# Both mixers of a two-layer encoder, ordered by the scheduler's other machine model

## The chip, the cores and the metric

The kernel runs on one core of one Trainium2 chip. The metric is the device time of one execution in microseconds. The core has five instruction streams that run side by side and meet at semaphores: TensorE (PE in the profile; PEld is its weight load), VectorE (DVE), ScalarE (ACT), GpSimd (POOL), and SyncE (SP), which issues all the DMAs here. Each of them takes its instructions in the order in which the compiled program lists them.

## The reference

The model is an encoder trunk with two layers on one sequence of 1024 tokens, each of 1024 float32 numbers. Each layer is a mixer and a SwiGLU, both with an RMSNorm ahead of them and a residual sum behind them.

```python
h = x
for layer in range(2):
    u = rms_norm(h, g_mix[layer])
    h = h + (mla_stick_breaking_mixer if layer == 0 else chunk_band_mixer)(u, ...)
    u = rms_norm(h, g_ffn[layer])
    h = h + (silu(u @ w_gate) * (u @ w_up)) @ w_down
return rms_norm(h, g_final)
```

The first mixer has two groups of eight heads. One group is latent attention (MLA): queries and keys come out of low-rank products with their own norms, and a rotary part is added; the softmax sees whole chunks of 64 tokens up to its own. The other is stick-breaking attention, strictly causal, without a softmax:

```python
log_keep = where(before, log_sigmoid(-z), 0)
log_between = cumsum(log_keep, reverse=True) - log_keep
w = where(before, exp(log_sigmoid(z) + log_between), 0)
```

The second mixer is attention with sixteen heads in which each chunk of 64 tokens sees itself and the eight chunks before it, with a learned bias per head and distance.

## The kernel before, in words

Everything is kept transposed, model dimension on the 128 partitions, tokens along the free dimension, in two halves of 512 tokens. A matrix product in nearly float32 precision is made of three products of rounded parts: `mm3` (L277 to L282) multiplies high by high, high by low and low by high, each a TensorE instruction of up to 512 columns. The parts come from `split` (L250): the high part is a rounding copy (`round_to`, L243, ScalarE or VectorE), the low part a subtraction (`rest`, L248, on VectorE or GpSimd as the caller says). `weight` (L267) loads a tile of weights from DRAM (L264) and splits it; `dense` (L284) is a row of `mm3` into one PSUM bank.

The program has four stages.

*The first mixer* (`mixer0`) starts with `start` (L351): for each of the 16 tiles of x a load, the scaled high part and low part (`feed`, L327 and L328), the value products of all heads, and the query and key products of the first two heads. Then come four rounds of stick-breaking attention, two heads each (`sb_step`): scores (L894, L895), a chain over VectorE, ScalarE and GpSimd (L897 to L904, with `rest` for the low part), the running sums as products with a triangle of ones (L916 to L921), the weights (L927, L928) and the products with the values (`weighted`, L831). Beside the rounds run the projections for later heads. Beside the fourth round runs `prepare`: the latent projections, their two norms (`feed`, `square_sum` L299 to L303, `rstd` L313 to L320, `columns` L343), the rotary part (L988 to L990), the first heads' keys (L1002, L1005) and the maximum of the first heads' scores (L1049, L1051; L1030, L1033, L1035). Then come four rounds of MLA attention (`mla_attend`, scores L1120 to L1122, exponentials L1123, sums L1072, denominators L1088) with the next heads' projections beside them, and the output projection (`out_half`) of the first half of the tokens beside the last round.

*The SwiGLU stages* (`ffn`) compute the hidden layer and the way down by a seven-product scheme (`Seven`). The second half of the mixer's output projection runs at their head. Their instructions are written out by hand as a list of steps.

*The second mixer* (`mixer1`) has eight rounds of two heads (`band_project`, `band_max` with L1175 and L1178, `band_attend` with L1201 to L1204), with the projections of later heads beside them.

**What sets the order.** Two things. In the code, `weave` (L785) draws from two generators, attention steps and dense products, by costs that are written by hand, and `step` (L764) puts a step's later parts behind the first parts of later steps: this gives the order in which the program is traced. Then, when the `TileContext` closes, the framework's scheduler plays the traced program on a model of the machine. For each engine it takes, among the instructions whose inputs are done and whose buffer is free at that moment of the model, the one that was traced first. So an instruction that the model sees as late is passed by others of its engine. The order that comes out for each engine is the program; buffers of a pool are handed out on the way. Costs of instructions enter through the model alone.

The body of each SwiGLU stage is exempt: inside `with self.pinned()` (L231) every instruction of TensorE, VectorE, ScalarE and GpSimd gets an edge to the one traced before it on its engine, so these keep the traced order:

```python
class PinnedCore:
    def __init__(self, tc):
        nc = tc.nc
        self.sync = nc.sync
        self.tensor, self.vector, self.scalar, self.gpsimd = (
            Pinned(tc, e) for e in (nc.tensor, nc.vector, nc.scalar, nc.gpsimd))
```

SyncE's DMAs are not wrapped, so their order is the scheduler's in all four stages. Behind the pinned body, each SwiGLU stage ends with the products of its last group (`add`, L706), which is scheduled freely, together with the head of what follows.

The function that the change touches is `kernel`, the last of the file:

## Time and profile before

| | us |
|---|---|
| three timed runs | 2590.89, 2594.2, 2595.98 |
| their median | 2594.2 |
| the profiled execution | 2591.68 |
| its span, first to last instruction | 2589.5 |

The profile is of one execution. "Busy" is the union of the records of an engine's instructions; records of TensorE overlap, since a product's record opens before the one ahead of it has closed. A line of groups gives the source line, the engine, what is written and read by the names in the code, shapes and count, then busy us and mean ns, then the idle time of the engine just before these instructions and what ended it. A line L243, L248 or L280 is that of a helper; L74 is the helper through which every pinned instruction is traced. The granted clock is TensorE's, as a share of full speed.

The stages lie at 0 to about 645 us (first mixer), to about 1340 us (first SwiGLU), to about 1880 us (second mixer), and to the end (second SwiGLU and the final norm).

### The profile page before, as it was taken

How to read it: one execution, taken by the hardware profiler on the slowest of the kernel's cores; microseconds unless marked ns; L12 is line 12 of the kernel's file. 1: busy time of each engine (PE TensorE's matmuls, PEld its weight loads, DVE VectorE, ACT ScalarE, POOL GpSimd, SP SyncE). 2: the span in 40 equal slices, each digit the busy share in tenths (PEclk: the TensorE clock that was granted, in tenths of full speed). 3: DMA queues.
4: the chain of work that ended last, by engine and by line, in shares of the span. 5: the costliest groups of instructions: out<-in, count | busy, mean ns of one | idle time of the engine just before them, and what ended most of it. 6: DMA issues, size and time to landing. Idle time of an engine off the chain costs nothing.

```text
span 2589.5 us, 33647 instructions
## 1 busy us (share of the span) xinstructions
PE 2513.1 (97%) x11758; PEld 1938.4 (75%) x11758; DVE 1890.9 (73%) x3072; ACT 1168.4 (45%) x2028; POOL 517.0 (20%) x489
## 2 busy tenths in 40 slices
PE   7999989999999999999999999999999999999997
PEld 6766766557778888888877777776777888888886
DVE  6888887665787666677765777777688766667776
ACT  4777676444454334433252433334444443444324
POOL 3333324653000000000031333335300000000004
PEclk9999999999999999999999999999999999999999
DMA  4221100124434344476652222223553434447661
GB/s 143 61 60 54 54 17 29 35 74 153 162 100 160 109 143 143 139 260 209 227 168 68 74 74 86 74 70 91 178 167 99 165 105 140 145 137 262 210 226 69
DMA packets 179432, 319.70 MB, mean 123 GB/s; under 512 B 20544, under 2 KB 36800, under 8 KB 179264
## 3 DMA queue, kind: packets, MB, share of 16 engines
q1 hardware_dynamic: 179264, 317.56, 37.2%
q8 instruction: 93, 1.52, 0.2%
q14 instruction: 75, 0.61, 0.1%
HBM read 222.58 MB, written 84.41 MB: 119 GB/s over the span
## 4 chain that ended last, share of the span: by engine, by line
PE 73%; DVE 8%; DMA 2%; ACT 1%; issue 1%; POOL 0%; DVEq 0%; SPq 0%; POOLq 0%; ACTq 0%
PE z L74 24%; PE mm L74 12%; PE o L74 6%; PE mm L280 6%; PE mm L281 6%; PE mm L282 6%; PE o L831 4%; DVE u L74 2%; PE z L1201 2%; PE z L1175 1%; PE z L1202 1%; PE z L1120 1%; DVE u L303 1%; PE z L1088 1%; PE z L1121 1%
## 5 line engine op out<-in xcount | busy, mean ns | idle before, releaser
L74 PE MATMUL z<-u,vh 128*128 128x512 f32 x976 | 304.0, 393 | 4.6 <-DVE u L74 4.6
L74 PE MATMUL z<-u,wh 128*128 128x512 f32 x976 | 302.2, 390 | 6.4 <-DVE u L74 6.4
L280 PE MATMUL mm<-u,wh 128*128 128x512 f32 x720 | 291.7, 405 | 2.9 <-DVE c L989 1.8
L281 PE MATMUL mm<-u,wh 128*128 128x512 f32 x720 | 284.1, 395 | 0.9 <-DVE u L248 0.9
L248 POOL TENSOR_TENSOR wl<-wr,wh 128x512 fp32r<-128x512 f32 (+2 forms) x95 | 122.0, 1289 | 809.2 <-ACT wh L243 739.0
L282 PE MATMUL mm<-u,wl 128*128 128x512 f32 x720 | 282.9, 393 | 0.0
L74 PE MATMUL mm<-u,wh 128*128 128x512 f32 x720 | 223.4, 392 | 4.5 <-ACT wh L74 4.5
L74 PEld LDWEIGHTS z<-u,wh 128*128 128x128 f32 x976 | 183.2, 188 | 47.3 <-DVE u L74 9.5
L74 PEld LDWEIGHTS z<-u,vh 128*128 128x128 f32 x976 | 184.4, 189 | 45.4 <-ACT u L74 6.2
L74 PE MATMUL z<-u,vl 128*128 128x512 f32 x488 | 191.1, 392 | 0.0
L74 PE MATMUL z<-u,wl 128*128 128x512 f32 x488 | 189.9, 389 | 0.0
L280 PEld LDWEIGHTS mm<-u,wh 128*128 128x128 f32 x720 | 135.5, 188 | 64.8 <-issue 40.3
L831 PE MATMUL o<-a,u 128*64 128x512 f32 (+3 forms) x768 | 171.8, 483 | 0.2 <-ACT a L1204 0.2
L74 PEld LDWEIGHTS mm<-u,wh 128*128 128x128 f32 x720 | 134.7, 188 | 35.7 <-ACT wh L74 6.9
L281 PEld LDWEIGHTS mm<-u,wh 128*128 128x128 f32 x720 | 135.8, 189 | 31.0 <-issue 6.8
L282 PEld LDWEIGHTS mm<-u,wl 128*128 128x128 f32 x720 | 135.6, 188 | 29.2 <-issue 2.1
L74 PE MATMUL mm<-u,vh 128*128 128x512 f32 x496 | 152.7, 389 | 0.0
L248 POOL TENSOR_TENSOR u<-wr,u 128x512 fp32r<-128x512 f32 x8 | 10.9, 1374 | 668.6 <-ACT u L243 668.6
L74 PE MATMUL mm<-u,wl 128*128 128x512 f32 x360 | 140.8, 391 | 0.8 <-DVE wl L74 0.5
L1204 ACT ACTIVATE a<-a 128x1024 f32<-128x1024 f32 (+3 forms) x96 | 70.6, 738 | 144.6 <-DVE a L1203 144.4
L74 ACT CAST vh<-vr 128x512 fp32r<-128x512 f32 (+1 forms) x166 | 95.9, 577 | 80.2 <-DVE vr L74 31.2
L1203 DVE TENSOR_TENSOR a<-z,bias 128x1024 f32<-128x1024 f32 (+3 forms) x96 | 78.8, 823 | 70.1 <-PE z L1202 54.7
(248 smaller groups left out, 5968.5 us busy)
## 6 DMA issues: line engine op xcount, KB each, us to landing
u<-f_t SPq DMA_DIRECT2D x144, 256.0 KB, 5.2
vr<-in_w_up SPq DMA_DIRECT2D x88, 256.0 KB, 4.2
wr<-in_w_gate SPq DMA_DIRECT2D x88, 256.0 KB, 3.6
f_t<-x SPq DMA_DIRECT2D x72, 256.0 KB, 2.0
wr<-in_w_out SPq DMA_DIRECT2D x64, 256.0 KB, 3.0
f_t<-e SPq DMA_DIRECT2D x54, 256.0 KB, 3.5
ld<-f SPq DMA_DIRECT2D x54, 256.0 KB, 5.2
h<-u SPq DMA_DIRECT2D x48, 256.0 KB, 2.4
```

Of the source, the lines that this page charges most:

```text
L74: return lambda *a, **k: self.tc.keep_in_program_order(f(*a, **k))
L248: self.eng(eng).tensor_tensor(lo, src, hi.bitcast(F32), ALU.subtract)
L280: mm(out, wh, xh, start=first, stop=False, skip_group_check=onto)
L281: mm(out, wh, xl, start=False, stop=False, skip_group_check=onto)
L282: mm(out, wl, xh, start=False, stop=last, skip_group_check=onto)
L303: self.eng(eng).tensor_tensor(acc, acc, sq, ALU.add)
L831: self.nc.tensor.matmul(o[rh, cs], vt[j // 4][:, j % 4, rh], w[:, e, cs], start=first, stop=last)
L1088: nc.tensor.matmul(den[64 * e:64 * e + 64, :], self.ones[:, 0:64], esum[:, e, :], start=True, stop=True)
L1120: mm(z[:, e, cs], kth[0:kr, bs], qh[0:kr, cs], start=True, stop=False)
L1201: mm(z[:, e, cs], ks[e][kh][0][:, bs], qs[e][hf][0][:, cs], start=True, stop=False)
L1203: nc.vector.tensor_tensor(ex[:, :, cs], z[:, :, cs], tk[:, :, xs], ALU.add)
L1204: nc.scalar.activation(ex[:, :, cs], ex[:, :, cs], AF.Exp)
```

## The change

The scheduler can play the program on either of two models of the machine. The default is used before; the other, a simulator of the engines' timelines, is chosen by one argument. It models with its own costs what an instruction takes, when its result can be used, how many instructions wait ahead of an engine, when a DMA lands, what a GpSimd operation takes, and TensorE's clock. The traced program is the same; the order of each engine's list and the handing out of buffers are the scheduler's under that model, wherever the code does not pin them.

```diff
-    with tile.TileContext(nc) as tc:
+    with tile.TileContext(nc, schedule_with_timeline_sim=True) as tc:
         tile_trunk(tc, args)
```

## The prediction

> **What bounds the kernel now.** I read the page first, then the busy time of each engine by stage, then what TensorE waited for, then ten-microsecond windows where its idle time is bunched. From the page, the span, the busy times and the engine shares of the chain of waits:
>
> ```profile
> span 2589.5 us, 33647 instructions
> ...
> PE 2513.1 (97%) x11758; PEld 1938.4 (75%) x11758; DVE 1890.9 (73%) x3072; ACT 1168.4 (45%) x2028; POOL 517.0 (20%) x489
> ...
> PE 73%; DVE 8%; DMA 2%; ACT 1%; issue 1%; POOL 0%; DVEq 0%; SPq 0%; POOLq 0%; ACTq 0%
> ```
>
> TensorE (PE) is busy 2513.1 of 2589.5 us, so all its idle time is 76.4 us, and VectorE (DVE) is the only other engine with a real share of the chain. An order of instructions adds and removes no work; what it can move is those 76.4 us, and how much new idle time it makes. Where they lie, by stage (start:end, length, then busy us and instructions of PE, PEld, DVE, ACT, POOL, granted TensorE clock, DMA share, GB/s):
>
> ```profile
> core 0: us, PE busy (x) PEld busy (x) DVE busy (x) ACT busy (x) POOL busy (x), PEclk, DMA share, GB/s
> 0.00:60.00 60.00, 45.65 (x264) 39.40 (x265) 41.46 (x50) 27.02 (x49) 24.98 (x25) 1.00 0.48 145
> 60.00:340.00 280.00, 273.30 (x1338) 199.29 (x1336) 240.62 (x306) 192.56 (x284) 98.95 (x127) 1.00 0.20 58
> 340.00:440.00 100.00, 89.12 (x349) 59.51 (x348) 85.79 (x106) 68.62 (x121) 37.40 (x31) 0.91 0.07 20
> 440.00:645.00 205.00, 199.30 (x878) 125.31 (x878) 130.65 (x167) 94.04 (x148) 109.59 (x76) 1.00 0.26 81
> 645.00:750.00 105.00, 98.16 (x416) 75.93 (x413) 89.06 (x141) 50.31 (x87) 0.00 (x0) 0.98 0.36 118
> 750.00:1160.00 410.00, 410.00 (x1810) 339.50 (x1809) 279.98 (x454) 168.82 (x310) 0.00 (x0) 1.00 0.47 162
> 1160.00:1260.00 100.00, 97.39 (x428) 80.01 (x428) 77.94 (x141) 32.67 (x66) 0.00 (x0) 1.00 0.66 227
> 1260.00:1340.00 80.00, 77.27 (x340) 62.66 (x339) 55.24 (x84) 33.80 (x58) 24.08 (x23) 1.00 0.55 178
> 1340.00:1880.00 540.00, 537.50 (x2871) 391.44 (x2870) 382.92 (x795) 212.05 (x375) 190.93 (x181) 1.00 0.30 91
> 1880.00:1980.00 100.00, 93.23 (x390) 73.01 (x389) 86.83 (x138) 48.42 (x84) 0.00 (x0) 0.98 0.35 118
> 2400.00:2500.00 100.00, 98.02 (x432) 80.54 (x431) 75.50 (x138) 30.38 (x61) 0.00 (x0) 1.00 0.62 214
> 2500.00:2590.00 90.00, 74.12 (x411) 64.00 (x409) 56.17 (x92) 36.17 (x71) 31.05 (x27) 0.95 0.33 111
> ```
>
> The first mixer (0 to 645 us) holds 14.4 + 6.7 + 10.9 + 5.7 = 37.6 us of the idle time, the second (1340 to 1880 us) only 2.5. The SwiGLU stages have no idle time in their long middle (750 to 1160 us) and 6.8 us at each start (645 to 750 and 1880 to 1980), the same twice, in instructions that are held in program order. What TensorE waited for, in total us, times and longest:
>
> ```profile
> PE z L282 <- DVE u L328: 7.3, 6, 1.7
> PE z L280 <- ACT wh L243: 5.8, 1, 5.8
> PE mm L280 <- DVE f L989: 3.5, 1, 3.5
> PE z L921 <- POOL c L248: 2.9, 4, 1.1
> PE z L1088 <- DVE b L1072: 2.9, 2, 1.5
> PE z L1033 <- DVE m L1030: 2.6, 1, 2.6
> ```
>
> These are small waits of one to three microseconds at the head of an in-order list: an instruction stands ahead of others although its operand is late. That is what another order can change. The 5.8 is the first load of the kernel, and stays.
>
> **The change part by part.** It removes and adds no instruction and no byte. It replaces the order of TensorE, VectorE, ScalarE and GpSimd in both mixers, in the last products of each SwiGLU stage (outside the pinned part), and of the DMA issues of SP everywhere, since those are pinned nowhere; buffers are handed out in the new order too. I price it stage by stage by the idle time, with both ends: all of a stage's idle time goes, or as much is added as a row of this trace shows for a stage of its kind.
>
> *Start, 0 to 60 us: idle 14.4 us, taken as -1.* Half of it is the first load and the ramp, 7.3 us are the six waits of the value products for the low part `u` of L328. Each low part hangs on a load, a cast and a subtraction that no order shortens; only another product can be put in front. Ends: -7 and +4 (half of it again).
>
> *Stick-breaking, 60 to 340 us: idle 6.7 us, taken as -3.* The waits for `c` of L248 and its like are about one microsecond each and have dense products as neighbours that could go first, so a model that knows the low part later puts them first. Ends: -6.7 and +6.7.
>
> *The latent projections, 340 to 440 us, taken as -4.* Here is the largest single piece:
>
> ```profile
> 300.00:310.00 10.00, 10.00 (x50) 8.11 (x49) 5.81 (x7) 5.21 (x7) 2.15 (x4) 1.00 0.17 53
> 310.00:320.00 10.00, 10.00 (x53) 7.93 (x50) 5.88 (x9) 5.24 (x9) 3.87 (x6) 1.00 0.12 38
> 320.00:330.00 10.00, 10.00 (x48) 7.37 (x48) 6.68 (x11) 5.70 (x10) 2.59 (x5) 1.00 0.08 27
> ...
> 360.00:370.00 10.00, 9.87 (x39) 6.50 (x38) 9.91 (x14) 6.80 (x10) 2.48 (x2) 1.00 0.00 0
> 370.00:380.00 10.00, 9.65 (x37) 5.31 (x36) 9.78 (x13) 7.70 (x12) 2.57 (x2) 1.00 0.01 2
> 380.00:390.00 10.00, 3.79 (x13) 2.21 (x12) 9.42 (x14) 6.36 (x10) 4.17 (x4) 0.60 0.00 0
> 390.00:400.00 10.00, 9.93 (x41) 7.51 (x41) 7.59 (x10) 8.55 (x22) 2.33 (x2) 0.88 0.23 72
> ...
> 420.00:430.00 10.00, 7.19 (x21) 5.58 (x22) 8.54 (x13) 5.12 (x9) 4.72 (x5) 0.66 0.07 20
> ```
>
> From 360 to 390 us VectorE is busy 29.1 of 30 us and TensorE loses 0.1 + 0.4 + 6.2 = 6.7 us behind it; from 300 to 330 us VectorE was busy only 18.4 of 30 us with TensorE full. So it is a bunching of VectorE work, not a lack of VectorE time. The idle time costs a second time: the granted clock falls to 0.60, 0.88 and 0.66, and the busy time in these three windows is worth 3.79 x 0.40 + 9.93 x 0.12 + 7.19 x 0.34 = 5.1 us less than at full clock. The stage is thus worth 10.9 + 5.1 = 16 us. An order can spread the bunch (-16) or make another like that of 360 to 400 us (6.7 + 1.5 + 1.2, about +9). A greedy order does not look ahead to the bunch, so I take a quarter of the gain.
>
> [...]
>
> *MLA attention, 440 to 645 us: idle 5.7 us, taken as -2*, by the argument of the stage before last. Ends: -5.7 and +5.7.
>
> *Second mixer, 1340 to 1880 us: idle 2.5 us, taken as +2.* There is next to nothing to win here. The cover is TensorE's own queue of ready dense products; if the new order has the share of idle time that 60 to 340 us has (2.4%), it is 12.9 us, +10.4 against now. Ends: -2.5 and +10.4; I take the low side because VectorE is busy only 382.9 of 540 us there.
>
> *The issues of SP, taken as 0.* Their waits, in total us, times and longest:
>
> ```profile
> SPq L264 <- POOL wl L248: 346.6, 88, 20.0
> SPq L264 <- DVE wl L248: 239.5, 66, 42.0
> ```
>
> The weight loads wait for their buffers, so a changed issue order mostly changes where SP waits. Behind a waiting load stand the moves of queries and keys and the loads of attention outputs. In the SwiGLU stages only 1160 to 1260 and 2400 to 2500 us have idle time in reach of a late load: 2.6 + 2.0, ends -4.6 and +4.6. The starts of those stages and the kernel's end I leave as they are: pinned, or a last chain that no order shortens.
>
> The sum is -1 - 3 - 4 - 2 + 2 + 0 = -8 us. The profiled execution took 2591.68 us (span 2589.5 and 2.2 around it), so it would take 2583.7; the median of the three timed runs is 2594.2, 2.5 us above the profiled one, so I predict 2586 for the median.
>
> **The rivals.** *The waits only move (2594).* As many waits arise as go, or the order hardly differs, since most of each engine's sequence is set by data and buffers and the SwiGLU stages are pinned; this is also the case in which the change does not do what it says. For it: every stage's gain above is a few microseconds, and the second mixer's +10.4 would by itself cancel the sum. Against it: the waits of the first mixer have ready neighbours.
>
> *Slower: VectorE bunches more (2613).* The mechanism is that of 360 to 400 us: VectorE serves attention steps, splits and the norm and rope chain from one in-order list, and an order that puts the chain's instructions where attention needs VectorE most makes TensorE wait and its clock fall. A piece costs about 9.4 us; two more pieces and none of the gains make 2594 + 19 = 2613. For it: VectorE is busy 240.6 of 280 and 85.8 of 100 us from 60 to 440 us, so it has 54 us to spare beside 18 of TensorE's. Against it: the spare time just before the bunch. It decides as soon as one piece comes without the sum's gain.
>
> A row that speaks to VectorE's length in any order, two groups of one operation and shape, from 60 to 645 us:
>
> ```profile
> L248 DVE TENSOR_TENSOR c<-b,c 128x512 fp32r<-128x512 f32 x24 | 24.3, 1014 | 2.4 <-ACT c L904 2.3
> L248 DVE TENSOR_TENSOR wl<-wr,wh 128x512 fp32r<-128x512 f32 x35 | 23.9, 691 | 3.7 <-ACT wh L243 3.5
> ```
>
> The `c` subtraction runs while GpSimd does the other half of the same pair, and takes 1014 ns for 691. An order that sets 24 such pairs apart in time saves VectorE 24 x 0.32 = 8 us, one that brings as many other subtractions beside GpSimd costs it as much; either is inside the ends of the stages. [...]
>
> *Larger gain (2566).* The bunch spreads wholly (-16) and the waits of 60 to 340 and 440 to 645 us go (-6.7 - 5.7): 2594 - 28 = 2566. For it: the spare VectorE time. Against it: that everything would have to go right at once.
>
> *Slower by TensorE's own order (about 2610).* From the page:
>
> ```profile
> L831 PE MATMUL o<-a,u 128*64 128x512 f32 (+3 forms) x768 | 171.8, 483 | 0.2 <-ACT a L1204 0.2
> ```
>
> The half-array products of L831 now overlap in twos: 768 records of 483 ns are 371 us, in 171.8 us of time. If one in ten of these 384 twos lost its overlap, that would be 38 x 0.4 = 15 us more. Nothing in the data forces the two apart, and they are neighbours in the code, so this is the least likely.
>
> **How the numbers follow.** Chances: the forecast 0.32, the larger gain 0.12, moved waits 0.21, VectorE's bunches 0.25, TensorE's order and others on that side 0.10. A measurement of this kernel can tell about 0.2%, 5.2 us, from no change: faster 0.44, the same 0.21, slower 0.35. The likeliest case alone runs from 2575 to 2589. The ends of all stages together are about -42 and +40 us; since they will not all fall to one side, and no more than 2 in 10 is to be left out, the range is 2564 (the larger gain) to 2622 (three bunches and no gain).
>
> **What would show it.** Right: TensorE's idle time of 60 to 645 us falls from 23.3 to about 14 us, the granted clock of 340 to 440 us rises over 0.91, the waits for `f` L989 and `m` L1030 are gone or under 1 us, and the second mixer stays under 5 us. Wrong: a stretch of 30 us or more with VectorE over 29 of 30 and TensorE under 24; idle time over 10 us in the second mixer; the time of L831 over 180 us; or a start of a SwiGLU stage that loses much more than 6.8 us, which would say that SP's order or a late end of the mixer counts and that the pinned parts are not out of reach.

## The result, and the profile after

The kernel after takes 2751.46 us (median of five runs, 2748.15 to 2753.26), the kernel before on the same chip 2594.2 us (five runs, 2590.89 to 2595.98). The ratio is 1.0604 with an interval from 1.0592 to 1.0615: 157 us slower. The forecast was 2586 us with a range up to 2622, so both the sign and the range were wrong. One of the four executions of experiment 13 took 8832 us at a mean granted clock of 0.28, for a reason that is not known, and the ratio given there leaves it out.

The page of the kernel after, with span, busy times, the busy tenths of TensorE and the granted clock in forty slices, and the engine shares of the chain of waits:

```profile
span 2746.4 us, 33800 instructions
...
PE 2564.8 (93%) x11758; PEld 1973.5 (72%) x11758; DVE 1894.4 (69%) x3072; ACT 1170.3 (43%) x2028; POOL 524.5 (19%) x489
...
PE   8998987889999999999999999888899999999997
...
PEclk9999998979999999999999999999899999999999
...
PE 77%; DVE 13%; ACT 4%; issue 3%; DMA 2%; POOL 1%; SPq 0%; DVEq 0%; POOLq 0%; ACTq 0%
```

No engine does other work: the counts are the same, and VectorE is busy 1894.4 us, before 1890.9. TensorE's idle time is 2746.4 - 2564.8 = 181.6 us in place of 76.4, which is 105 us. Its busy time is 51.7 us longer for the same 11758 records of products, at a lower granted clock (0.960 on the mean in place of 0.994). The two make the 157 us.

The windows by stage of the kernel after, cut where TensorE has done about as many instructions as at the cuts shown of before (columns as there: start:end, length, then busy us and instructions of PE, PEld, DVE, ACT, POOL, granted clock, DMA share, GB/s):

```profile
0.00:60.00 60.00, 48.24 (x286) 41.37 (x286) 41.73 (x52) 26.88 (x49) 22.88 (x23) 1.00 0.48 149
60.00:360.00 300.00, 274.96 (x1313) 202.25 (x1311) 231.49 (x294) 187.25 (x275) 96.19 (x125) 0.96 0.19 53
360.00:481.00 121.00, 93.69 (x353) 62.91 (x354) 101.32 (x121) 74.79 (x130) 40.16 (x35) 0.89 0.07 19
481.00:719.00 238.00, 211.82 (x892) 137.99 (x891) 132.84 (x162) 97.12 (x148) 111.12 (x75) 0.89 0.22 72
719.00:827.00 108.00, 98.45 (x399) 76.13 (x398) 88.36 (x140) 49.75 (x86) 0.00 (x0) 0.94 0.32 108
...
1412.00:2037.00 625.00, 568.86 (x2881) 406.98 (x2879) 378.66 (x798) 212.34 (x377) 200.08 (x181) 0.93 0.25 79
```

Stick-breaking is 300 us long in place of 280, the latent projections 121 in place of 100, MLA attention 238 in place of 205, and the second mixer 625 in place of 540: 20 + 21 + 33 + 85 = 159 us. What lies between the mixers is 693 us long in place of 695, and 709 us follow the second mixer in both. So the whole change is in the two mixers, and more than half of it in the second, in which the prediction saw next to nothing to win and little to lose. There the idle time went from 2.5 to 56.1 us.

What TensorE waited for in the kernel after (total us, times, longest):

```profile
PE z L1033 <- DVE m L1030: 19.7, 11, 2.4
PE z L1175 <- DVE m L1178: 14.6, 8, 2.6
PE mm L280 <- DVE u L245: 12.9, 4, 4.1
PE o L831 <- ACT a L1204: 10.8, 13, 1.6
PE o L831 <- POOL a L888: 9.9, 7, 5.1
```

Four of these five belong to attention steps: the product that turns the row maxima (L1033), the row maxima's own products that wait for a PSUM bank which VectorE has yet to read (L1175), and value products that wait for an exponential or a mask (L831). In the list shown of before L1033 stood with 2.6 us, and the row of L831 there had 0.2 us of idle time.

A round of the second mixer (two heads) shows where they come from. The lists of TensorE for one round, before and after, from the program itself (d: dense product of a later head, S: score L1201 or L1202, M: row maximum L1175, N: L1033, b: value product L831, o: denominator L1088; a number counts the neighbours of one kind; in the profile each of the float32 products N, b and o leaves two records):

```
before  S d2 S2 d S d15 b2 o2 S4 d6 M2 d6 M2 d3 b2 S4 d3 M2 d4 M2 d2 b2 d S4 M2 d2 M2 b2 d3 M2 d5 M2 d12 N2
        S d b S2 b d S o2 d3 S4 d14 b2 S4 d18 b2 S4 d21 b2 S4 M2 d9 b2 S4 M2 d27 b2 S4 M2 d21 b2 S4 M2 d9 b2 d3 N2
after   S d21 S2 d S o2 d21 S4 d b2 d17 M2 d5 M2 d6 b2 d17 S4 M2 d24 M2 d4 b2 d3 S4 d7 M4 b2 M4 N2
        S4 o2 S4 b2 S8 b2 S4 b2 M2 S4 b2 M2 b2 S4 d20 M2 d b2 S4 b2 d16 M2 d3 b2 d25 N2
```

The same 192 dense products stand in a round. In the kernel before they lie between the attention products to its end; in the kernel after they come earlier, the last eight of the sixteen maxima ahead of the first N are without any, and so are the 44 attention products behind it. The windows of that round, first of the kernel before (the two that hold its sixteen maxima), then of the kernel after (the last four of six, and the sum of all six):

```profile
1455.00:1467.00 12.00, 12.00 (x58) 8.63 (x58) 5.89 (x12) 4.58 (x8) 3.00 (x4) 1.00 0.31 99
1467.00:1479.00 12.00, 12.00 (x60) 7.98 (x59) 11.34 (x38) 4.04 (x7) 2.67 (x3) 1.00 0.32 88
```

```profile
...
1554.00:1566.00 12.00, 12.00 (x72) 9.14 (x72) 6.98 (x13) 4.97 (x8) 1.85 (x1) 1.00 0.22 68
1566.00:1578.00 12.00, 10.86 (x85) 9.29 (x83) 7.97 (x20) 3.42 (x6) 5.91 (x5) 1.00 0.14 45
1578.00:1590.00 12.00, 7.60 (x22) 3.31 (x23) 8.14 (x22) 1.18 (x2) 3.33 (x4) 0.63 0.30 97
1590.00:1602.00 12.00, 11.02 (x49) 5.54 (x47) 8.32 (x17) 6.78 (x15) 7.25 (x6) 0.80 0.15 45
sum 72.00, PE 65.48 PEld 45.50 DVE 43.38 ACT 22.89 POOL 23.99; mean PE 10.91 PEld 7.58 DVE 7.23 ACT 3.82 POOL 4.00
```

Before, VectorE is busy 11.34 of 12 us in the stretch of the maxima, and TensorE is full at full clock, since dense products stand between them. After, TensorE has run through its dense products by 1576 us; in the next 12 us it is busy 7.60 us and its clock is 0.63, and in the bare stretch behind that 0.80. The round is 72 us long in place of 60: 6.5 us of idle time, and most of the rest by the clock (7.60 x 0.37 + 11.02 x 0.20 = 5.0 us).

The timeline of TensorE there (start, duration, count of joined products, and in brackets the idle time ahead and what ended it):

```profile
1576.05 0.76 PE L1175 MATMUL z<-u,u 128*128 128x256 f32 x4
1577.95 0.44 PE L831 MATMUL o<-a,u 128*64 128x128 f32 x4 [1.15 <-ACT a L1204]
1580.85 1.76 PE L1175 MATMUL z<-u,u 128*128 128x128 f32 x4 [2.46 <-DVE m L1178]
1584.45 1.02 PE L1033 MATMUL z<-ident,m 128*4 128x128 f32 x4 [1.85 <-DVE m L1030]
```

The first mixer looks alike, with other names. In the kernel after, two windows of the stick-breaking stage in which the list of TensorE has no dense product, and the largest sum of waits from 240 to 300 us:

```profile
250.00:260.00 10.00, 4.14 (x18) 2.62 (x18) 7.46 (x9) 5.86 (x8) 5.69 (x8) 0.67 0.18 42
260.00:270.00 10.00, 8.96 (x32) 5.23 (x31) 5.73 (x9) 5.15 (x10) 3.35 (x6) 0.64 0.01 2
```

```profile
PE o L831 <- POOL a L888: 7.1, 3, 5.1
```

### The profile page after: what moved, and what is told of

It is laid out like the page before. It is cut to its first block, busy times and chain, and to the rows that moved or that the text cites. A ratio compares the mean times of both kernels' runs of the same rounds, so it can differ in the third digit from the quotient of the medians.

```text
span 2746.4 us, 33800 instructions
## 1 busy us (share of the span) xinstructions
PE 2564.8 (93%) x11758; PEld 1973.5 (72%) x11758; DVE 1894.4 (69%) x3072; ACT 1170.3 (43%) x2028; POOL 524.5 (19%) x489
## 4 chain that ended last, share of the span: by engine, by line
PE 77%; DVE 13%; ACT 4%; issue 3%; DMA 2%; POOL 1%; SPq 0%; DVEq 0%; POOLq 0%; ACTq 0%
PE z L74 23%; PE mm L74 12%; PE mm L280 8%; PE mm L281 8%; PE mm L282 7%; PE o L74 6%; PE o L831 4%; DVE u L74 2%; PE z L1201 1%; PE z L1088 1%; PE z L1202 1%; PE z L1175 1%; DMA wr<-in_w_down 1%; DVE z L1178 1%; POOL b L1072 1%
## 5 line engine op out<-in xcount | busy, mean ns | idle before, releaser
L280 PE MATMUL mm<-u,wh 128*128 128x512 f32 x720 | 292.1, 407 | 30.8 <-DVE u L245 12.9
L282 PE MATMUL mm<-u,wl 128*128 128x512 f32 x720 | 287.1, 399 | 0.0
L280 PEld LDWEIGHTS mm<-u,wh 128*128 128x128 f32 x720 | 137.9, 192 | 84.8 <-issue 25.8
L831 PE MATMUL o<-a,u 128*64 128x512 f32 (+3 forms) x768 | 161.0, 502 | 24.6 <-ACT a L1204 10.8
L74 PEld LDWEIGHTS mm<-u,wh 128*128 128x128 f32 x720 | 136.9, 191 | 35.5 <-ACT wh L74 5.8
L281 PEld LDWEIGHTS mm<-u,wh 128*128 128x128 f32 x720 | 138.4, 192 | 32.7 <-issue 4.0
L74 PE MATMUL mm<-u,wl 128*128 128x512 f32 x360 | 142.1, 395 | 0.6 <-DVE wl L74 0.3
L248 POOL TENSOR_TENSOR u<-wr,u 128x512 fp32r<-128x512 f32 x8 | 10.4, 1310 | 684.1 <-ACT u L243 684.1
L1178 DVE CUSTOM_DVE_ANT_0 z<-z,bias 128x384 f32<-128x384 f32 (+3 forms) x192 | 93.6, 502 | 53.1 <-PE z L1175 50.8
L1072 POOL TENSOR_TENSOR b<-b,a 128x512 f32<-128x512 f32 (+3 forms) x80 | 114.2, 1428 | 82.5 <-ACT a L1204 66.7
```

Source lines behind the costliest of these rows:

```text
L74: return lambda *a, **k: self.tc.keep_in_program_order(f(*a, **k))
L248: self.eng(eng).tensor_tensor(lo, src, hi.bitcast(F32), ALU.subtract)
L280: mm(out, wh, xh, start=first, stop=False, skip_group_check=onto)
L281: mm(out, wh, xl, start=False, stop=False, skip_group_check=onto)
L282: mm(out, wl, xh, start=False, stop=last, skip_group_check=onto)
L831: self.nc.tensor.matmul(o[rh, cs], vt[j // 4][:, j % 4, rh], w[:, e, cs], start=first, stop=last)
```

## The experiments

All of them hold or release lists; 7 and 8 also leave out a part of VectorE's work. TensorE is held to a list by edges between neighbours that carry no semaphore, put in after tracing and ahead of the scheduler:

```python
places = ...                      # the wanted list: places in the traced order
for a, b in zip(places[:-1], places[1:]):
    tc.add_manual_dep(mine[b], mine[a].name, <edge without semaphore>, reason="fix_order")
```

Two theories stood at the start. Theory A: the loss is TensorE's own list, in which dense products run ahead and attention is left without cover. Theory B: it is something else that the other model decides, namely the lists of the other engines, SyncE's DMAs, or the hand-out of buffers.

**1. The default model with TensorE's list of the kernel after.**

```diff
+        fix_order(tc, {"tensor": <list of the kernel after>})
     (scheduler: default)
```

> The default model, as before, but TensorE's instructions are held in exactly the order that they have in the changed kernel; every other engine and the DMAs are ordered by the default model around it. Theory A (TensorE's order is the cause: dense projection products run ahead of the attention steps that they should cover, so the end of each attention round stands alone): 2751 us within 25, and rounds of about 72 us in the second mixer. Theory B (the cause is the order of VectorE, ScalarE, GpSimd and the DMAs under the other model, bunches of VectorE work as in my rival): under 2640 us, since those engines are back under the default model.

Measured: 2820.88 us, ratio 1.0869 (1.0849 to 1.0888). TensorE's list alone, without the other model, brings the whole loss, and 69 us more than that: what else differs from the kernel after, the other engines' lists and the hand-out of buffers under the default model, fits this list less well. Theory B falls as an explanation of the loss; the size that A gave was too small.

**2. The other model with TensorE's list of the kernel before.**

```diff
-    with tile.TileContext(nc) as tc:
+    with tile.TileContext(nc, schedule_with_timeline_sim=True) as tc:
         tile_trunk(tc, args)
+        fix_order(tc, {"tensor": <list of the kernel before>})
```

> The other model, but TensorE's instructions are held in exactly the order of the kernel before. Theory A: 2594 us within 15, rounds of 60 us in the second mixer. Theory B: over 2700 us, since VectorE, ScalarE, GpSimd and the DMAs keep the other model's order.

Measured: 2621.32 us, ratio 1.0106 (1.0091 to 1.0121). With all other engines free, 130 of the 157 us are gone. The 27 us that stay are outside A's band. By the trace the first mixer is 24 us longer (it ends at 670.7 us in place of 646.7) and the second 11 (540.2 us from its first product to its last, in place of 529.6), with a few us less elsewhere. Two rows of this run's waits, both of the first mixer for the most part:

```profile
PE o L343 <- DVE u L320: 9.9, 2, 9.3
PE z L1033 <- DVE m L1030: 9.2, 4, 5.3
```

**3 and 4. The other model with TensorE held near the traced order.** An instruction of TensorE may not pass the one that was traced 84, or 16, places ahead of it. In the kernel before no product stands more than 84 places ahead of its traced place.

```diff
+    for k in range(n, len(mine)):          # TensorE; n = 84 or 16
+        tc.add_manual_dep(mine[k], mine[k - n].name, <edge without semaphore>)
```

> The other model, but no TensorE instruction may be issued before the one traced 84 places ahead of it on TensorE (84 is how far one ran ahead in the kernel before). The mean lead of the second mixer's dense products falls from 42 places to 21. Theory A: the loss follows the lead, so about half of it stays, 2640 to 2700 us. Theory B: 2740 us or more.

> The same with a window of 16 places: mean lead 2.5 places in the second mixer and 4.4 in the first, as in the kernel before (2.7 and 3.5). Theory A: 2585 to 2615 us. Theory B: over 2700 us.

Measured: 2721.33 us (1.0474 to 1.0505 times before) with 84 places, 2758.16 us (1.0618 to 1.0651) with 16. The mean lead of the dense products of the second mixer over the traced order is 41.7 places in the kernel after, 20.9 with 84, 2.5 with 16, and 2.7 in the kernel before. So the loss does not follow the mean lead, and A in that form falls. What the list with 84 places has in common with that of the kernel after shows in a round: there too, the last maxima and the first N stand bare (`d4 b2 M4 N2`, where the kernel before has `M2 d5 M2 d12 N2`). With 16 places the last maxima have dense products beside them (`M2 d2 b M2 d2 b N2`), eight earlier ones stand without (`M4 S4 b2 M4`), and a round still takes about 66 us. Three windows of the run with 84 places around such a place:

```profile
1618.00:1623.00 5.00, 1.90 (x15) 1.45 (x14) 4.83 (x12) 2.30 (x5) 0.84 (x1) 0.93 0.19 52
1623.00:1628.00 5.00, 3.15 (x10) 1.70 (x11) 3.65 (x13) 0.00 (x0) 0.00 (x0) 0.50 0.14 39
1628.00:1633.00 5.00, 5.00 (x18) 2.76 (x17) 1.49 (x2) 1.04 (x2) 0.41 (x2) 0.54 0.23 92
```

VectorE is at its limit (4.83 of 5 us), TensorE has nothing else in its list, and the clock falls to 0.50. That suggested theory M: the price is paid at the sixteen maxima of a round, at VectorE's pace, wherever the dense products are listed ahead of them. Its rival R: the scores that stand bare behind the maxima cost it.

**5. The kernel before with only these dense products moved.**

```diff
-  d6 M2 d6 M2 d3 b2 S4 d3 M2 d4 M2 d2 b2 d S4 M2 d2 M2 b2 d3 M2 d5 M2 d12 N2
+  d47 M4 b2 S4 M4 b2 S4 M4 b2 M4 N2    (the attention products as before, the dense ones ahead)
```

> The default model, TensorE held in the order of the kernel before with one edit: in each round of the second mixer the dense products that stand between the first of the sixteen row-maximum products of the second token half (L1175) and the product that turns the maxima (L1033) are listed ahead of the first of the sixteen; 330 products move, at most 58 in a round, nothing else. Theory M (the sixteen maxima of a round go at VectorE's pace, 15.9 us busy of 17 in this stretch before; listing the round's dense products ahead of them leaves TensorE nothing to run while it waits for banks, and its clock falls): 6 to 10 us in each of seven rounds, 2635 to 2665. Rival R (what costs is the scores and exponentials that are left without cover at the end of a round, not the maxima): the products that follow the maxima keep their cover here, so 2585 to 2605.

Measured: 2657.02 us, ratio 1.0247 (1.0231 to 1.0262), inside M's band. 330 dense products listed ahead of the maxima instead of between them, and nothing else, cost 63 us: the second mixer takes 592.9 us in place of 529.6 (first to last of its products). Windows of one round of this run, the maxima and what follows them:

```profile
1545.00:1562.00 17.00, 12.97 (x63) 8.20 (x62) 12.95 (x41) 2.91 (x5) 2.00 (x2) 1.00 0.21 65
1562.00:1574.00 12.00, 12.00 (x39) 6.63 (x37) 6.23 (x9) 5.39 (x9) 2.56 (x5) 0.72 0.15 52
```

4.0 us are lost as idle time at the maxima, and 12 x 0.28 = 3.4 us by the clock behind them, where dense products already stand in the list again.

**6. The kernel after with these maxima covered again.** The 66 dense products of that stretch are spread evenly over its attention products.

```diff
-  M2 d5 M2 d6 b2 d17 S4 M2 d24 M2 d4 b2 d3 S4 d7 M4 b2 M4 N2
+  M d3 M d2 M d2 M d2 b d2 b d3 S d2 S d2 S d2 S d2 M d3 M d2 ... M d2 M d2 N2
```

> The other model, TensorE held in the order of the kernel after with one edit: in each round of the second mixer the dense products that stand between the first of the sixteen row-maximum products and L1033 (66 of them) are spread evenly over the attention products of that stretch, where the kernel after lists them first and the last eight maxima bare. Theory M: the waits there (1.1 + 2.5 + 1.8 us in a round) go, and the low clock behind them (0.71 over the next 17 us, worth about 5 us) with them, 6 to 10 us in each of six or seven rounds: 2685 to 2715. Rival R (the bare scores behind are what costs): their waits come back behind L1033, 2735 to 2755.

Measured: 2754.83 us, ratio 1.0625 (1.0610 to 1.0641). It gives nothing, as R said. But the edit has a fault that experiment 9 brought out: it splits groups of products, and that has a price of its own (the 48 records of L831 in a round make 11.9 us here, from 1606 to 1677 us, and 10.0 in the kernel after, from 1602 to 1673).

**7 and 8. Half of VectorE's maxima left out, in either list.** The maxima L1178 of every second head are left out, and a memset stands for them.

```diff
+        nc.vector.memset(m2[:, 1, :, :], 0.0)
-                for e in range(2):
+                for e in range(1):
                     nc.vector.tensor_tensor_reduce(out=z[:, e, :n], ...   # L1178
```

> The other model, TensorE held in the order of the kernel after; VectorE's biased maxima (L1178) are left out for every second head, which takes 96 of 192 of them and their reads, 61 us of VectorE's work, 8 us in a round, 5 of them among the sixteen; a memset of 64 bytes a partition stands for their result. TensorE's instructions and order are those of the kernel after. Theory M (VectorE's pace at the bare maxima is what TensorE waits for): 5.4 us of waits in a round shrink to 1 to 2 and the clock falls less: 25 to 50 us less than the kernel after, 2700 to 2725. If what is lost is not VectorE's pace there: 2740 to 2755.

> The same omission (L1178 for every second head, 61 us of VectorE's work) with the default model and TensorE held in the order of the kernel before. Theory M: the maxima lie beside dense products there, so 61 us of VectorE's work less is worth 0 to 8 us: 2584 to 2596. If the time of the second mixer is VectorE's pace in this order too: 20 to 50 us less, 2545 to 2575.

Measured: 2729.92 us in the list of the kernel after (1.0518 to 1.0549 times before, 21.5 us less than the kernel after by the medians, 18 by the ratios), and 2591.13 us in that of the kernel before (0.9980 to 0.9999, 2.5 us less). The instructions left out took 61 us; VectorE's busy time as a whole fell by 47 us in the one list and by 37 in the other. The same omission is worth about 20 us in one list and 2.5 in the other. This is what "covered" means here. That is under M's band of 25 to 50: VectorE's pace at the maxima is a part of the loss, and not all of it.

**9 and 12. The kernel after with the round covered to its end.** From 110 places ahead of the first of the sixteen maxima to the end of the bare stretch, the 158 dense products are spread evenly over the 94 attention products. In 9 they are spread over single products; in 12 the four scores of a tile, the two maxima, the two L831, the two L1088 and the two N stay together. The first mixer keeps the list of the kernel after.

```diff
 9:
+  ... S d2 S d S d2 S d b d2 b d2 M d M d2 M d2 M ... N d2 N d2 S d S d2 ...
 12:
+  ... d5 S4 d4 o2 d4 S4 d5 b2 d4 M2 d5 M2 d4 b2 ... M2 d4 N2 d5 S4 d4 o2 d4 S4 d5 b2 ...
```

> The other model, TensorE held in the order of the kernel after with one edit, in rounds 0 to 6 of the second mixer: from 110 places ahead of the first of the sixteen row-maximum products to the end of the attention products that stand bare in the kernel after, the dense products of that stretch (158 in a round) are spread evenly over its attention products (94); the order within the dense and within the attention products stays. The first mixer keeps the order of the kernel after. Theory C (a round takes 71.4 us instead of 59.8 only since its dense products are spent before its attention is through, whichever attention stands bare): the rounds fall to 60 to 63 us, 2751 - 7 x 9 to 11 = 2675 to 2700. If the loss sits in the other engines' order or in the hand-out of buffers under this model: 2735 to 2755.

> As the run before with the round covered to its end (e9: 158 dense products of a round spread evenly over 94 attention products, other model, first mixer as in the kernel after), but the attention products move in groups that stay whole: the four products of a score tile, the two of a row maximum, the two of L831 and of L1088, the two of L1033. Changes between float32 products (L831, L1088, L1033) and the others are 242 in the second mixer, against 240 in the kernel after and 436 in e9. Theory C (dense cover missing at the end of a round makes 9 to 12 us a round; e9 paid it back with L831 at 16.6 us a round for 9.5 and L1088 at 4.3 for 2.1): rounds of 60 to 63 us, 2670 to 2700. If cover is not what is missing: 2735 to 2760.

Measured: 9 takes 2791.45 us (1.0754 to 1.0786), 40 us more than the kernel after; 12 takes 2711.02 us (1.0439 to 1.0468), 40 us less. In 9 the low clock is gone from these rounds, and they are longer all the same. One whole round of 9, then three of its groups in that round:

```profile
1612.00:1687.00 75.00, 71.48 (x327) 45.46 (x327) 42.85 (x92) 23.05 (x41) 21.49 (x23) 1.00 0.20 63
```

```profile
L831 PE MATMUL o<-a,u 128*64 128x384 f32 (+3 forms) x48 | 16.6, 458 | 0.0
...
L1175 PE MATMUL z<-u,u 128*128 128x384 f32 (+3 forms) x24 | 7.3, 316 | 1.8 <-DVE a L1203 1.1 <-DVE m L1178 0.8
...
L1088 PE MATMUL z<-b,ones 128*64 128x512 f32 x8 | 4.3, 618 | 0.0
```

The same groups in a round of the kernel before, and of 12:

```profile
L831 PE MATMUL o<-a,u 128*64 128x128 f32 (+3 forms) x48 | 9.5, 458 | 0.0
...
L1088 PE MATMUL z<-b,ones 128*64 128x512 f32 x8 | 2.1, 605 | 0.0
```

```profile
L831 PE MATMUL o<-a,u 128*64 128x384 f32 (+3 forms) x48 | 9.1, 458 | 1.2 <-ACT a L1204 1.2
L1088 PE MATMUL z<-b,ones 128*64 128x512 f32 x8 | 2.2, 618 | 0.0
```

The 48 records of L831 are the two each of 24 products. One record lasts 458 ns in all three, 22.0 us for the 48; but two neighbouring products that write the two halves of a bank run side by side (from 1490 us of the kernel before the records of the two begin at 1490.188 and 1490.194 and last 643 ns each), and the 24 take 9.5 us, against 16.6 us when a dense product stands between the two. L831 and L1088 together make 9.3 us a round, and that is the most of the 11.5 us by which 71.48 us of busy time at full clock exceed the 60 us of a round before. With the groups whole (12) a round takes 64.1 us.

The lengths of a round, first dense product to first dense product of the next, as the mean of five rounds:

| list of TensorE | round, us | time, us |
|---|---|---|
| before | 59.8 | 2594.2 |
| 5: before, dense ahead of the maxima | 68.1 | 2657.0 |
| after | 71.1 | 2751.5 |
| 13: after, maxima covered, groups whole | 68.2 | 2742.3 |
| 12: after, whole round covered, groups whole | 64.1 | 2711.0 |
| 9: after, whole round covered, groups split | 75.7 | 2791.5 |

So 7.0 of the 11.3 us by which a round grew come back when its dense products are put between its attention products again. 12 is 11 us above the band of theory C; in its round TensorE is still idle 2.9 of 64 us, and its clock is 0.97:

```profile
1589.00:1653.00 64.00, 61.06 (x328) 44.43 (x328) 44.23 (x93) 23.00 (x41) 21.79 (x23) 0.97 0.24 75
```

An even spread is not the spread of the kernel before, which has twelve dense products between the last maximum and N; an even one has four, and N waits 1.0 us there.

**13. Experiment 6 again, with the groups whole.**

```diff
+  M2 d6 M2 d5 b2 d5 S4 d5 M2 d5 M2 d5 b2 d5 S4 d5 M2 d5 M2 d5 b2 d5 M2 d5 M2 d5 N2 S4 o2 S4 b2 S8 ...
```

> As the run with the maxima covered again (e6: the 66 dense products between the first of the sixteen row maxima and L1033 spread evenly, other model), but with the groups kept whole. Theory M (VectorE's pace at the bare maxima is the whole of it): 2685 to 2715. Theory C (the cover is only moved inside the round, and the scores behind L1033 stay bare and at a low clock): 2725 to 2755.

Measured: 2742.25 us, ratio 1.0563 (1.0544 to 1.0583): 9 us less than the kernel after, in the band of C and far from M's. Covering the maxima alone leaves the scores behind them bare. Theory M is a part of the answer, and C the larger one: a round's dense products are one stock, and where the list spends it early, the attention products at the other end go at the pace of VectorE and ScalarE, with TensorE's clock falling on top (in a round of this run, from 1601 to 1669 us, TensorE waits 4.8 us for VectorE and 0.6 for ScalarE, and its clock is 0.95). It is not shown to be the whole: in 12 a round is still 4.3 us longer than in the kernel before.

**10. The other model with TensorE's and VectorE's lists of the kernel before.**

```diff
+        fix_order(tc, {"tensor": <list of before>, "vector": <list of before>})   # other model
```

> The other model with TensorE and VectorE both held in their orders of the kernel before; ScalarE, GpSimd and SyncE are free. The run with TensorE alone held took 2621.3, 27 us above before, most of it waits of 2.7 to 9.3 us for VectorE at 340 to 460 us and around 560 us. Theory V (VectorE's order under this model makes the rest): 2590 to 2606. If it is ScalarE's, GpSimd's or SyncE's order: 2613 to 2630.

Measured: 2603.44 us, ratio 1.0039 (1.0024 to 1.0054). Of the 27 us that experiment 2 left, 18 are VectorE's list: the second mixer is 530.3 us long again, the first ends at 660.7. The rest, 9 us, is with ScalarE, GpSimd, SyncE or the buffers and was not taken apart.

**11. The default model with TensorE held to 16 places of the traced order**, the same hold as in 4.

> The default model, TensorE held to 16 places of the traced order: the same hold with which the other model took 2758.2. Theory C (the hold is harmless, and the other model uses those 16 places to put dense products ahead of the row maxima): 2590 to 2625. If the hold itself loses the time: over 2700.

Measured: 2670.20 us, ratio 1.0310 (1.0287 to 1.0333), between the two bands. The hold itself costs 76 us, the other model inside it 88 more. So 4 was not a clean test of the lead, and where its 88 us are lost was not taken apart. It also says that the default model's long steps are worth something: with the hold the first mixer ends at 686.1 us in place of 646.7.

**14. Fewer changes of kind in the list of the kernel before.** L831, L1088 and L1033 are float32, all other products of the round are rounded parts. In the second mixer of the kernel before the pace of the products beside a change of kind, less the median pace of their own line and shape, makes 0.19 us for each of 126 changes from float32 and 0.21 us for each of 124 changes to it.

```diff
-  b2 o2 S4 d6 M2 d6 M2 d3 b2 S4 ...  d14 b2 S4 d18 b2 S4 d21 b2 S4 M2 d9 b2 ...
+  b4 o2 S4 d6 M2 d6 M2 d3 S4 ...     d14 S4 d18 b4 S4 d21 S4 M2 d9 b4 ...
```

> The default model, TensorE in the order of the kernel before with one edit in the second mixer: 39 pairs of value products (L831) wait for the next pair of the same output bank (20 places on the mean) and stand ahead of it, so that changes between float32 products and the others fall from 253 to 175 there. Nothing else moves. Theory S (each change costs about 0.2 us, as the pace of the products beside a change shows: 0.19 us from float32, 0.21 us to it): 78 x 0.2 = 16 us less, 2574 to 2584. Rival (the exponentials' three buffers of a come free later, and ScalarE and the scores wait for them): 2590 to 2615.

Measured: 2592.03 us, ratio 0.9992 (0.9983 to 1.0001): no difference that can be told. By the same reckoning the changes took 33.9 us in the second mixer in place of 50.0, 16 us less. Theory S is not borne out by the time, which lies in the rival's band. Waits came, of the scores (L1201) above all, as the rival said; that the buffers of `a` are behind them was not looked into. TensorE's waits in the second mixer, of this run and then of the kernel before:

```profile
PE z L1201 <- DVE m L1178: 3.6, 6, 0.6
PE z L1033 <- DVE m L1030: 1.9, 6, 0.3
PE z L1175 <- DVE m L1178: 1.7, 2, 1.0
PE z L1201 <- DVE a L1203: 1.3, 3, 0.7
```

```profile
PE z L1088 <- DVE b L1072: 1.4, 1, 1.4
PE z L1175 <- DVE m L1178: 0.5, 1, 0.5
```

In all they are 10.4 us in 20 waits in place of 2.3 us in 4, 8 us more. The stage was 2.1 us shorter (527.5 us), so some 6 of the 16 us are not accounted for, and the price of a change stays a reckoning from neighbours.

**15. The kernel after with the first mixer's list of the kernel before.**

```diff
+        fix_order(tc, {"tensor": <list of before in the first mixer, of after elsewhere>})   # other model
```

> The other model, TensorE held in the order of the kernel after, but in the first mixer in the order of the kernel before. Theory C (each mixer loses by its own order of TensorE): the first mixer loses what it lost with TensorE wholly in the order of before (e2, about 25 us) instead of 75, so 2751 - 50 = 2690 to 2712. If the first mixer's loss is the other engines' order or the hand-out of buffers: 2735 to 2755.

Measured: 2705.05 us, ratio 1.0429 (1.0411 to 1.0446). The first mixer ends at 676.6 us in place of 721.5, the second is as long as in the kernel after (618.9 us, 614.7 there). So the two mixers lose separately: about 46 us of the loss are the first mixer's list of TensorE and, with experiment 2, another 84 us are the second's.

Moving dense products back between the attention products of the first mixer, as in 12, was not tried. For the first mixer the reason "cover spent ahead" is thus read from its windows and argued by likeness; that it is TensorE's list is shown. Why the other model takes attention steps as late, and so lists dense products ahead of them, was not looked into. No run with all the kernel's work was measurably faster than the kernel before.

## Why the prediction was wrong

**What bounds the kernel** was read rightly: no engine's work changed, and the result is idle time of TensorE (105 us) and longer busy time at a lower clock (52 us).

**Start, -1:** idle time there went from 14.4 to 11.8 us. Right in sign and inside its ends.

**Stick-breaking, -3, ends of 6.7 us to either side:** it came to +20 us. The argument was that the waits have dense neighbours "that could go first". They did go first, and by the windows that is the fault: they were then missing later, where the list has attention alone (0.67 granted and 4.14 of 10 us busy at 250 to 260 us).

**Latent projections, -4, between -16 and +9:** +21. Two of the signs named for it came true in this stage and told nothing: no wait for `f` of L989 is over 0.8 us (three, 2.3 us in all), and none for `m` of L1030 is left. Others stand in their place, with the dense products of L280 waiting 3.7 us for `c` of L1002 and 3.6 us for `c` of L989, and the clock is 0.89. The waits for `m` of L1030 grew elsewhere: 5.3 us in MLA attention and 14.4 in the second mixer. The prediction also counted the fall of the clock in the kernel before as a second cost of the 6.2 us of idle time from 380 to 390 us. In finer windows the clock was 1.00 from 381 to 382 us and 0.53 from 382 to 383, after a wait of 1.42 us; the longest wait, 3.48 us for `f` of L989, began at 383.05, when it was low already.

**MLA attention, -2, ends of 5.7:** +33, by the argument of stick-breaking; that its fault is the same one is argued, not shown.

**The second mixer, +2, between -2.5 and +10.4:** +85. This is the step that failed worst. It said that "the cover is TensorE's own queue of ready dense products", which is right, and then priced losing it by the idle share of another stage. That row is of a stage whose cover is in place; it is no bound on a stage without cover. It also took "the low side because VectorE is busy only 382.9 of 540 us there". That is a mean over rounds; in the 12 us of a round's maxima VectorE was busy 11.34 us even then. A bound could have been had from such a window: about 8 us lost at bare maxima in each of seven rounds is what experiment 5 measured.

**SyncE's issues, 0:** right. The stages between and behind the mixers are as long as they were.

**The rivals.** *VectorE bunches more* named the right chain of effects (TensorE waits behind VectorE, its clock falls, some 9 us a piece; a round grew by 11.3 us) and a wrong origin. With TensorE's list of the kernel before, VectorE's list under the other model costs 18 us (2 against 10), near the 19 that this rival was given; 130 of the 157 us are TensorE's list. The sign that was named for it is there around 390 to 420 us (VectorE busy 29.49 us, TensorE 21.98), but the kernel before has it too: the prediction's own rows of 360 to 390 us add up to 29.11 and 23.31. And it was given two more pieces, where there are eight rounds in the second mixer alone. *TensorE's own order*, by L831 losing its overlap, did not happen in the kernel after. (Its 384 "twos" count records; with two records a product they are 192 pairs.)

```profile
L831 PE MATMUL o<-a,u 128*64 128x512 f32 (+3 forms) x768 | 161.0, 502 | 24.6 <-ACT a L1204 10.8 <-POOL a L888 9.9 <-ACT a L928 3.3
```

161.0 us stay under the 180 that were named as the sign. Experiment 9 made it happen, and there a round's value products took 16.6 us in place of 9.5. *A larger gain* and *moved waits* fell.

**The ends.** The sum of all upper ends was +40 us, and the change cost 157. Each end was taken as the stage's present idle time or as that of a neighbour, which assumes that an order can only shift the waits that are there. The case that was missing is that an order takes away what hides a wait, and the waits that are hidden do not show as waits in any view of the kernel before.

## What to carry to other kernels

When an order is to change, price the cover and not the waits: slice a stage into its rounds, find the windows in which another engine is near its limit while TensorE is full, and ask what a round costs if the independent products that lie there stood earlier. Spread such products to the end of the round, but keep together the products that overlap in pairs: covering a round gained 40 us with the groups whole and lost 40 us with the groups split (and even the first is 117 us above the kernel before). To tell an order's effect from the rest of what a scheduler does, hold one engine to the other kernel's list, both ways round.

## What the runs showed of the hardware

In these rows the granted clock fell after waits of 1.15 to 2.9 us. In the kernel after it was 1.00 from 1580 to 1581 us and 0.62 from 1581 to 1582, after waits of 1.15 and 2.46 us with 0.44 us of products between them; the wait of 1.85 us came when it was 0.50 already. In experiment 3 it was 0.93 from 1618 to 1623 us, where TensorE was busy 1.90 of 5 us, and 0.50 from 1623 to 1628; the longest wait of that round was 2.9 us. In experiment 9 it stayed at 1.00 from 1652 to 1662 us, where TensorE was busy 6.57 of 10 us, through waits of 1.1, 0.8 and 1.6 us with dense products in between. What decides whether it falls, no run here shows.

The overlap of two products of L831 showed only for neighbours in the list: the 24 value products of a round took 9.5 us in pairs (396 ns each; kernel before) and 16.6 us with other products between them (692 ns each; experiment 9). A change between float32 products and the others took, by an estimate from the pace of the products beside it in the kernel before, 0.19 us of TensorE's time from float32 and 0.21 us to it; the run with 78 fewer changes was not measurably faster (experiment 14).
